# Stationary operands moved to the start address modulo 256 bytes of the moving ones, by sizes of small tiles

## The chip, the cores and the metric

The kernel runs on one core of one Trainium2 chip. The metric is the device time in microseconds (us) of one execution. The engines are TensorE (PE; its weight loads have a row of their own, PEld), VectorE (DVE), ScalarE (ACT), GpSimd (POOL) and SyncE (SP), which issues most of the loads. TensorE has two granted clocks here, 1.2 and 2.4 GHz; a granted clock of 1.00 in the rows is the upper one.

## The reference, cut to what matters

One decoder layer on 256 tokens of width 2048, in float32: a layer norm, one wide projection, three token mixers (a short gated convolution A, a chunked spatial gating B, a conformer convolution C), each projected back and multiplied by a sigmoid gate, an output projection with a residual and a layer norm, and a SwiGLU feed-forward net of inner width 5632 with a residual and a layer norm.

```python
x = layer_norm(x, ln_in_g, ln_in_b)
z = jnp.einsum('bsd,de->bse', x, w_in[l])
a_b, a_c, a_h, b_u, b_v, c_a, c_g, g = jnp.split(z, SPLITS, axis=-1)
gates = jax.nn.sigmoid(g + gate_bias[l]).reshape(bsz, s, N_BRANCH, D_MODEL)
y_a = short_gated_conv(a_b, a_c, a_h, conv_a_w[l])
y_b = chunked_spatial_gating(b_u, b_v, sg_ln_g[l], sg_ln_b[l], sg_w[l], sg_b[l])
y_c = conformer_conv(c_a, c_g, cc_conv_w[l], cc_conv_b[l], cc_ln_g[l], cc_ln_b[l])
proj = jnp.einsum('bsnc,ncd->bsnd', jnp.stack([y_a, y_b, y_c], axis=2), w_branch[l])
mix = jnp.einsum('bsd,de->bse', jnp.sum(gates * proj, axis=2), w_out[l])
x = layer_norm(DEEPNORM_ALPHA * x + mix, ln_mix_g[l], ln_mix_b[l])
h_gate, h_up = jnp.split(jnp.einsum('bsd,df->bsf', x, w_ffn_in[l]), 2, axis=-1)
ffn = jnp.einsum('bsf,fd->bsd', jax.nn.silu(h_gate) * h_up, w_ffn_out[l])
x = layer_norm(DEEPNORM_ALPHA * x + ffn, ln_ffn_g[l], ln_ffn_b[l])
```

## The kernel before

**Products.** Every float32 factor is split into two float32r halves, a high one (ACT casts it, line 127 for weights) and a low one (DVE subtracts, line 129). A product is three matmuls of 128x512 into one PSUM bank: high by high, high by the weights' low, low by the weights' high (lines 197 to 199 in `mm_tile`, 243 to 245 in `product`). The *moving* operand is always a half of a weight tile, `whi` or `wlo`. The *stationary* operand, which a weight load of its own (LDWEIGHTS) brings into the array before each matmul, is a 128x128 block, 512 bytes in each partition, of the transposed activations: `th`/`tl` (halves of the layer's input, of the merged branches, of the normed input of the feed-forward net, of its inner activations), `yh`/`yl` (halves of a mixer's output), and the token sums `sum0`/`sum1` and `xS0`/`xS1`, with which some pairs of blocks are multiplied in seven products in place of eight. Transposes (line 305, `transpose4`) are matmuls of 128x128 by the constant `ident`.

**Stages.** The input projection and the gates read the first `th`/`tl` (to 819 us). Six blocks, one for each half of the output of each branch projection, read `yh`/`yl`. The gate and up projections of the feed-forward net come in three parts, from 819, 1080 and 1336 us, and read the second kind of `th`/`tl`, the list `x2T`, and the sums `xS`. After each part its down projection reads `th`/`tl` and `sum` at the old places. The weights stream through: SP loads them in the order of use, ACT and DVE split them some steps ahead, and PE takes them in program order. Beside that, DVE has a background list (convolution taps, line 558).

**Where tiles lie.** A pool hands out addresses in the order in which its tiles are first asked for, each rounded up to 32 bytes. `brp` (opened in `more_params`) holds what the mixers need: `merged0`, `tok`, `pad`, `cv`, `gate`, the statistics `bst0` and `bst1`, `yh`, `yl`, `merged1`. `ffp` (opened in `open_ffn`, after `brp` and `cwp` are closed) holds `x2T`, the residual `R`, `xS` and the tiles `a`.

Of the kernel before, what the change touches and what calls it, by code (L numbers as in the profile page):

```python
# [8 lines left out]
F32 = mybir.dt.float32  # L9
# [5 lines left out]
P = 128  # L15
D = 2048
S = 256
NT = S // P
DA = D // 2
KC = 31  # L20
# [32 lines left out]
def trunk_kernel(ctx: ExitStack, tc: tile.TileContext, x, ln_in_g, ln_in_b, w_in, gate_bias,  # L53
# [9 lines left out]
    small = ctx.enter_context(tc.tile_pool(name="small", bufs=4))  # L63
# [13 lines left out]
    def cols(j, w=NW):  # L77
        return slice(j * w, (j + 1) * w)

    def new_tmp():  # L80
        return tmp.tile([P, NW], F32, name="tmp")

    def blocks(ap):
        return ap.rearrange("p (b d) -> p b d", d=P)
# [119 lines left out]
    def defer(fn, after=DEFER, banks=True):  # L204


        deferred.append((clock[0] + after, fn, banks))
# [7 lines left out]
    def gemm(key, xs, evac, skew=0):  # L215

        first_tile, nk = chunk[key]
        xh, xl = xs
        ps = [acc_bank() for _ in range(NT)]
        n = nk // KT  # L220
        for i in range(n + skew):
            if i < n:
                pump(first_tile + i)
            for t, ii in ((0, i), (1, i - skew)):
                if not 0 <= ii < n:
                    continue
                hi, lo = split_t[first_tile + ii]
                for kk in range(KT):
                    k = ii * KT + kk
                    mm_tile(ps[t], xh, xl, t, k, hi, lo, kk, k == 0, k == nk - 1)  # L230
                if ii == n - 1:
                    if t == NT - 1:
                        halves.reverse()
                    evac(t, ps[t])
            clock[0] += 1
            run_deferred()
        for i in range(n):
            split_t.pop(first_tile + i)
# [62 lines left out]
    def transpose4(src):  # L301

        tp = tp_bank()
        for b in range(4):
            nc.tensor.transpose(out=tp[:, b, :], in_=src[:, b, :], identity=ident)  # L305
        return tp
# [16 lines left out]
        nc.gpsimd.tensor_tensor(out=rs, in0=r, in1=mhalf, op=ALU.pow)  # L323
        return mv[:, 0:1], rs

    def stats_tile(name, n, pool=None):
        return [(pool or small).tile([P, n, 6], F32, name=f"{name}{t}", bufs=1) for t in range(NT)]


    wi = w_in[0]  # L330
# [79 lines left out]
    def pcol(base, b):  # L410
        return prm[:, base + b:base + b + 1]
# [28 lines left out]
    def new_xt(pool):  # L440
        return (pool.tile([P, 16, S], F32R, name="th"), pool.tile([P, 16, S], F32R, name="tl"))
# [51 lines left out]
    br = ExitStack()  # L493
    brp = None
    cc_tok, cc_stats = [], stats_tile("cst", 2)
    b_ln, wT = [], []

# [28 lines left out]
    def branch_c_chunk(j):  # L526
        sig, st = {}, {}

        def evac_cg(t, ps):
            sig[t] = new_tmp()  # L530
            nc.scalar.activation(out=sig[t], in_=ps, func=AF.Sigmoid)

        gemm(("cg", j), xT, evac_cg, skew=SKEW_IN if j == 0 else 0)

        def evac_ca(t, ps):
            y = new_tmp()
            nc.vector.tensor_tensor(out=y, in0=ps, in1=sig[t], op=ALU.mult)

            def later():
                if t == 0:  # L540
                    st["pad"] = brp.tile([P, 4, KC - 1 + S], F32, name="pad", bufs=2)
                    nc.vector.memset(st["pad"][:, :, 0:KC - 1], 0.0)
                tp = transpose4(blocks(y))
                nc.scalar.copy(out=st["pad"][:, :, KC - 1 + t * P:KC - 1 + (t + 1) * P], in_=tp)
                if t == NT - 1:
                    queue_conv(st["pad"])
            defer(later)

        def queue_conv(pad):
            def tap(q, b):  # L550
                if q == 0 and b == 0:
                    st["cv"] = brp.tile([P, 4, S], F32, name="cv", bufs=2)
                cv, w_ = st["cv"], cw[:, 4 * j + b, q:q + 1]
                if q == 0:
                    nc.vector.tensor_scalar(out=cv[:, b, :], in0=pad[:, b, 0:S], scalar1=w_,
                                            scalar2=pcol(PR_CB, 4 * j + b), op0=ALU.mult, op1=ALU.add)
                else:
                    nc.vector.scalar_tensor_tensor(out=cv[:, b, :], in0=pad[:, b, q:q + S], scalar=w_,  # L558
                                                   in1=cv[:, b, :], op0=ALU.mult, op1=ALU.add)

            def back():
                if not cc_tok:
                    cc_tok.extend(brp.tile([P, DA], F32, name="tok", bufs=2) for _ in range(NT))
                for t in range(NT):
                    tp = transpose4(st["cv"][:, :, cols(t, P)])
                    dst = cc_tok[t][:, cols(j)]
                    nc.scalar.copy(out=blocks(dst), in_=tp)
                    nc.vector.bn_stats(out=cc_stats[t][:, j, :], in_=dst)

            for q in range(KC):  # L570
                for b in range(4):
                    background.append(lambda q=q, b=b: tap(q, b))
            background.append(lambda: defer(back))

        gemm(("ca", j), xT, evac_ca)
# [27 lines left out]


    vt = {(t, j): brp.tile([P, NW], F32, name="gate", bufs=4) for t in range(NT) for j in range(2)}
    bst = stats_tile("bst", 2, brp)
    for j in range(2):
        def evac_bv(t, ps, j=j):
            nc.scalar.copy(out=vt[t, j], in_=ps)
# [36 lines left out]
    def total(ps, add):  # L646

        if add is None:
            return ps
        c = new_tmp()  # L650
        nc.vector.tensor_tensor(out=c, in0=ps, in1=add, op=ALU.add)  # L651
        return c
# [67 lines left out]
    ac, pads, cvs = {}, {}, {}  # L720
# [10 lines left out]
    def evac_ah(i, t, h, ps, add):  # L731
        u = ac[t, h]
        nc.vector.tensor_tensor(out=u, in0=total(ps, add), in1=u, op=ALU.mult)

        def later():
            if h not in pads:
                pads[h] = brp.tile([P, 4, KC - 1 + S], F32, name="pad", bufs=2)
                nc.vector.memset(pads[h][:, :, 0:KA - 1], 0.0)
            pad = pads[h]
            tp = transpose4(blocks(u))  # L740
            nc.scalar.copy(out=pad[:, :, KA - 1 + t * P:KA - 1 + (t + 1) * P], in_=tp)
            if t < NT - 1:
                return
            cv = cvs[h] = brp.tile([P, 4, S], F32, name="cv", bufs=2)
            for q in range(KA):
                for b in range(4):
                    w_ = cw[:, 4 * h + b, KC + q:KC + q + 1]
                    if q == 0:
                        nc.vector.tensor_scalar(out=cv[:, b, :], in0=pad[:, b, 0:S], scalar1=w_,
                                                scalar2=None, op0=ALU.mult)  # L750
                    else:
                        nc.vector.scalar_tensor_tensor(out=cv[:, b, :], in0=pad[:, b, q:q + S], scalar=w_,
                                                       in1=cv[:, b, :], op0=ALU.mult, op1=ALU.add)
        defer(later, DEFER + i)
# [30 lines left out]
    ffp = None  # L785
    R, x2T, xS = [], [], []

    def open_ffn():
        nonlocal ffp
        br.close()  # L790
        cwx.close()
        ffp = ctx.enter_context(tc.tile_pool(name="ffp", bufs=1))
        x2T.extend(new_xt(ffp))
        R.extend(ffp.tile([P, D], F32, name=f"R{t}") for t in range(NT))
        xS.extend(ffp.tile([P, 4, S_PAIRS, P], F32R, name=f"xS{i}") for i in range(2))

    defer(open_ffn, 1)

    def bcast(src, j):
        t_ = new_tmp()  # L800
        nc.gpsimd.dma_start(out=t_, in_=src[0:1, cols(j)].broadcast_to([P, NW]))
        return t_

    stm = stats_tile("stm", 4)
    lg2, lb2 = (a.rearrange("(o d) -> o d", o=1) for a in (ln_in_g, ln_in_b))
    def residual_rows(j):
# [152 lines left out]
```

## Time and profile before

| | before |
|---|---|
| time, median of 3 runs | 1544.6 us (1544.12 to 1544.81) |
| the profiled execution: its time | 1543.98 us |
| its span, first to last instruction | 1541.9 us |
| PE busy | 1522.0 us of the span, 6799 matmuls |
| DVE busy | 1343.1 us |
| ACT busy | 771.6 us |
| mean DMA rate | 200 GB/s |

A matmul's duration in the rows is from its start until its result is complete, and matmuls overlap: one of 389 ns is followed after some 227 ns by the next. So a busy PE says little; what counts is the distance from start to start, and where one group of matmuls is longer than another of the same shape by some nanoseconds, its distance is longer by about as much.

### The profile page before, as it was taken

What the parts mean: (1) busy time and instruction counts of PE and PEld (TensorE: products, weight loads), DVE (VectorE), ACT (ScalarE), POOL (GpSimd) and SP (SyncE); (2) the same over time, 40 slices, a digit from 0 to 9 for tenths busy, and PEclk for the clock granted to TensorE, in tenths of its full rate; (3) what the DMA queues carried; (4) which work ended last, traced back from release to release, by engine and by line L of the source; (5) the groups of instructions that cost most, each with busy time, mean ns of one, the idle gap of its engine ahead of it and who ended that gap; (6) DMA issues with size and microseconds to landing.
All of it is one profiled execution on the core that took longest, in us unless ns stands there. A gap on an engine that the chain in (4) does not pass through costs nothing.

```text
span 1541.9 us, 18855 instructions
## 1 busy us (share of the span) xinstructions
PE 1522.0 (99%) x6799; PEld 1247.5 (81%) x6799; DVE 1343.1 (87%) x1792; ACT 771.6 (50%) x885; POOL 40.6 (3%) x72
## 2 busy tenths in 40 slices
PE   8999999999999999999999999999999999999997
PEld 5888888888888888888887888888888888888885
DVE  7699999978789878778979799998899998889677
ACT  6544445444455454545536455554555554455451
POOL 1000000000000000000101000000000000000001
PEclk9999999999999999999999999999999999999999
DMA  7766657566665655756766666676665656666663
GB/s 240 256 193 190 182 169 231 170 204 198 198 194 177 229 191 166 262 172 219 255 196 181 203 191 219 190 233 198 186 197 172 213 196 204 202 193 197 213 190 124
DMA packets 102549, 308.14 MB, mean 200 GB/s; under 512 B 9909, under 2 KB 11029, under 8 KB 102455
## 3 DMA queue, kind: packets, MB, share of 16 engines
q1 hardware_dynamic: 98006, 293.29, 60.0%
q0 software_dynamic: 3520, 11.54, 2.7%
q10 hardware_dynamic: 928, 2.11, 0.4%
q8 instruction: 53, 0.87, 0.2%
q14 instruction: 42, 0.34, 0.1%
HBM read 304.80 MB, written 2.10 MB: 199 GB/s over the span
## 4 chain that ended last, share of the span: by engine, by line
PE 86%; DVE 9%; issue 2%; DMA 1%; ACT 1%; POOL 0%; POOLq 0%; DVEq 0%; ACTq 0%
PE acc L243 24%; PE acc L245 24%; PE acc L244 24%; DVE cv L558 4%; PE acc L198 4%; PE acc L199 4%; PE acc L197 4%; DVE wlo L129 2%; PE acc L305 2%; DMA wraw<-in_w_in_dram 0%; DMA x<-in_x_dram 0%; POOL ve L320 0%; DVE st L468 0%; DVE tmp L635 0%; ACT whi L127 0%
## 5 line engine op out<-in xcount | busy, mean ns | idle before, releaser
L127 ACT CAST whi<-wraw 128x1024 fp32r<-128x1024 f32 x551 | 575.8, 1052 | 519.8 <-PE acc L245 274.0
L129 DVE TENSOR_TENSOR wlo<-wraw,whi 128x1024 fp32r<-128x1024 f32 x551 | 666.6, 1220 | 125.7 <-ACT whi L127 119.3
L243 PE MATMUL acc<-whi,th 128*128 128x512 f32 x1235 | 485.7, 393 | 0.0
L244 PE MATMUL acc<-wlo,th 128*128 128x512 f32 x1235 | 481.7, 390 | 0.0
L245 PE MATMUL acc<-whi,tl 128*128 128x512 f32 x1235 | 481.1, 390 | 0.0
L245 PEld LDWEIGHTS acc<-whi,tl 128*128 128x128 f32 x1235 | 231.8, 188 | 50.3
L243 PEld LDWEIGHTS acc<-whi,th 128*128 128x128 f32 x1235 | 231.9, 188 | 48.3 <-ACT th L311 0.5
L244 PEld LDWEIGHTS acc<-wlo,th 128*128 128x128 f32 x1235 | 232.1, 188 | 47.8
L197 PE MATMUL acc<-whi,th 128*128 128x512 f32 x496 | 195.1, 394 | 0.1
L199 PE MATMUL acc<-whi,tl 128*128 128x512 f32 x496 | 194.1, 392 | 0.0
L198 PE MATMUL acc<-wlo,th 128*128 128x512 f32 x496 | 193.8, 392 | 0.0
L127 ACT CAST whi<-tsum 128x1024 fp32r<-128x1024 f32 x114 | 95.2, 835 | 153.2 <-DVE tsum L139 98.8
L129 DVE TENSOR_TENSOR wlo<-tsum,whi 128x1024 fp32r<-128x1024 f32 x114 | 108.7, 953 | 20.2 <-ACT whi L127 19.7
L199 PEld LDWEIGHTS acc<-whi,tl 128*128 128x128 f32 x496 | 93.4, 188 | 20.4 <-DVE tl L312 0.8
L197 PEld LDWEIGHTS acc<-whi,th 128*128 128x128 f32 x496 | 93.5, 189 | 19.9 <-ACT th L311 0.6
L198 PEld LDWEIGHTS acc<-wlo,th 128*128 128x128 f32 x496 | 93.4, 188 | 19.4 <-DVE wlo L129 0.2
L558 DVE SCALAR_TENSOR_TENSOR cv<-pad,cw,cv 128x256 f32<-128x256 f32 x240 | 102.0, 486 | 0.0
L139 DVE TENSOR_TENSOR tsum<-tsum,wraw 128x512 f32<-128x512 f32 x114 | 78.1, 685 | 0.7
L243 PE MATMUL acc<-whi,yh 128*128 128x512 f32 x192 | 76.3, 398 | 0.0
L245 PE MATMUL acc<-whi,yl 128*128 128x512 f32 x192 | 75.9, 395 | 0.0
L244 PE MATMUL acc<-wlo,yh 128*128 128x512 f32 x192 | 75.9, 395 | 0.0
L651 DVE TENSOR_TENSOR tmp<-acc,tmp 128x512 f32<-128x512 f32 x92 | 59.9, 683 | 0.6
(164 smaller groups left out, 1178.1 us busy)
## 6 DMA issues: line engine op xcount, KB each, us to landing
wraw<-in_w_in_dram SPq DMA_DIRECT2D x208, 512.0 KB, 4.3
wraw<-in_w_ffn_in_dram SPq DMA_DIRECT2D x176, 512.0 KB, 4.5
wraw<-in_w_ffn_out_dram SPq DMA_DIRECT2D x88, 512.0 KB, 4.7
wraw<-in_w_branch_dram SPq DMA_DIRECT2D x48, 512.0 KB, 5.1
wraw<-in_w_out_dram SPq DMA_DIRECT2D x32, 512.0 KB, 5.8
tmp<-in_gate_bias_dram POOLq DMA_DIRECT2D x12, 256.0 KB, 4.4
R<-in_x_dram POOLq DMA_DIRECT2D x8, 256.0 KB, 8.6
x<-in_x_dram SPq DMA_DIRECT2D x2, 512.0 KB
```

Of the source, the lines that this page charges most:

```text
L127: nc.scalar.copy(out=hi, in_=t)
L129: nc.vector.tensor_tensor(out=lo, in0=t, in1=hi.bitcast(F32), op=ALU.subtract)
L139: nc.vector.tensor_tensor(out=out, in0=a, in1=b, op=ALU.add)
L197: nc.tensor.matmul(ps, lhsT=xh[:, k, ts], rhs=hi[:, kk, :], start=first, stop=False)
L198: nc.tensor.matmul(ps, lhsT=xh[:, k, ts], rhs=lo[:, kk, :], start=False, stop=False)
L199: nc.tensor.matmul(ps, lhsT=xl[:, k, ts], rhs=hi[:, kk, :], start=False, stop=last)
L243: nc.tensor.matmul(ps, lhsT=ah, rhs=bh, start=first, stop=False)
L244: nc.tensor.matmul(ps, lhsT=ah, rhs=bl, start=False, stop=False)
L245: nc.tensor.matmul(ps, lhsT=al, rhs=bh, start=False, stop=last)
L305: nc.tensor.transpose(out=tp[:, b, :], in_=src[:, b, :], identity=ident)
L558: nc.vector.scalar_tensor_tensor(out=cv[:, b, :], in0=pad[:, b, q:q + S], scalar=w_, in1=cv[:, b, :], op0=ALU.mult, op1=ALU.add)
L651: nc.vector.tensor_tensor(out=c, in0=ps, in1=add, op=ALU.add)
```

## The change

Four sizes in the two pools change, so that tiles that come later start elsewhere. No instruction is added or taken out, and the order of the instructions on each engine, the semaphores that they wait for and the shapes that they compute on are those of before. The tiles `pad` have rows of 288 in place of 286 elements, of which the last two aren't used; the two statistics tiles `bst0` and `bst1` (each 48 bytes, rounded up to 64) become slices of one of 256 bytes; `ffp` begins with an unused tile of 64 bytes.

```diff
-    def stats_tile(name, n, pool=None):
-        return [(pool or small).tile([P, n, 6], F32, name=f"{name}{t}", bufs=1) for t in range(NT)]
+    def stats_tile(name, n):
+        return [small.tile([P, n, 6], F32, name=f"{name}{t}", bufs=1) for t in range(NT)]
...
-                    st["pad"] = brp.tile([P, 4, KC - 1 + S], F32, name="pad", bufs=2)
+                    st["pad"] = brp.tile([P, 4, KC + 1 + S], F32, name="pad", bufs=2)
...
-    bst = stats_tile("bst", 2, brp)
+    bst_ = brp.tile([P, 64], F32, name="bst")
+    bst = [bst_[:, 12 * t:12 * t + 12].rearrange("p (j s) -> p j s", s=6) for t in range(NT)]
...
-                pads[h] = brp.tile([P, 4, KC - 1 + S], F32, name="pad", bufs=2)
+                pads[h] = brp.tile([P, 4, KC + 1 + S], F32, name="pad", bufs=2)
...
         ffp = ctx.enter_context(tc.tile_pool(name="ffp", bufs=1))
+        ffp.tile([P, 16], F32, name="align")
         x2T.extend(new_xt(ffp))
```

What that does to the start addresses in a partition, read from the two built programs (in bytes; in brackets modulo 256):

| tile | read by matmuls as | before | after |
|---|---|---|---|
| `whi`, `wlo` | moving | 38080 and on, 66752 and on (192) | same |
| `th`, `tl` outside `x2T` | stationary | 101568, 117952 (192) | same |
| `sum0`, `sum1` | stationary | 134336, 138432 (192) | same |
| `th`, `tl` of `x2T` | stationary | 159616, 176000 (128) | 159680, 176064 (192) |
| `xS0`, `xS1` | stationary | 208768, 214912 (128) | 208832, 214976 (192) |
| `yh`, `yl` | stationary | 202752, 210944 (0) | 202944, 211136 (192) |
| `a` (four buffers) | stationary of transposes | 221056 and on (128) | 221120 and on (192) |
| `merged0` | the same | 160704 (192) | same |
| `merged1` | the same | 219136 (0) | 219328 (192) |
| `gate`, `cv`, `R` | the same | (128) | (192) |
| `ident` | moving of transposes | 16512 (128) | same |

Within a tile the blocks start at multiples of 512 bytes (stationary) and 2048 bytes (moving), so that a tile's place modulo 256 is that of all its blocks.

## Rows read from the trace of the kernel before

**Rows 1.** The page, part 1, and the span with the granted clock.
```profile
PE 1522.0 (99%) x6799; PEld 1247.5 (81%) x6799; DVE 1343.1 (87%) x1792; ACT 771.6 (50%) x885; POOL 40.6 (3%) x72
...
core 0: 1541.9 us, clock 0.996
```
**Rows 2.** Waits of PE, longest first: engine, line, releaser, us, times, longest.
```profile
PE acc L305 <- DVE tmp L427: 5.9, 6, 2.0
```
**Rows 3.** Groups of PE by shape, 270.7 to 312.6 us (gate projection, first th/tl).
```profile
L244 PE MATMUL acc<-wlo,th 128*128 128x512 f32 x54 | 21.0, 389 | 0.0
L243 PE MATMUL acc<-whi,th 128*128 128x512 f32 x54 | 21.0, 389 | 0.0
L245 PE MATMUL acc<-whi,tl 128*128 128x512 f32 x53 | 20.6, 389 | 0.0
```
**Rows 4.** The same, 313 to 335 us (a branch projection, yh/yl).
```profile
L243 PE MATMUL acc<-whi,yh 128*128 128x512 f32 x32 | 12.7, 396 | 0.0
L244 PE MATMUL acc<-wlo,yh 128*128 128x512 f32 x32 | 12.7, 396 | 0.0
L245 PE MATMUL acc<-whi,yl 128*128 128x512 f32 x31 | 12.3, 396 | 0.0
```
**Rows 5.** The same, 1091 to 1166 us (gate and up projections, th/tl of x2T, xS).
```profile
L243 PE MATMUL acc<-whi,th 128*128 128x512 f32 x86 | 33.7, 392 | 0.0
L244 PE MATMUL acc<-wlo,th 128*128 128x512 f32 x85 | 33.5, 394 | 0.0
L245 PE MATMUL acc<-whi,tl 128*128 128x512 f32 x86 | 33.4, 388 | 0.0
L244 PE MATMUL acc<-wlo,xS 128*128 128x512 f32 x24 | 9.5, 394 | 0.0
```
**Rows 6.** Timeline of PE: first matmuls of three blocks (start us, duration us).
```profile
270.72 0.39 PE L243 MATMUL acc<-whi,th 128*128 128x512 f32 x1
...
312.89 0.40 PE L243 MATMUL acc<-whi,yh 128*128 128x512 f32 x1
...
335.29 0.39 PE L243 MATMUL acc<-whi,th 128*128 128x512 f32 x1
```
**Rows 7.** Busy time of PE (count) in the three gate and up stages.
```profile
818.90:993.60 174.70, 174.16 (x775) 1.00 0.64 198
1079.90:1249.30 169.40, 169.40 (x750) 1.00 0.63 197
1335.80:1465.30 129.50, 129.50 (x576) 1.00 0.62 196
```
**Rows 8.** Groups beside transposes: 996.1 to 1009 us, then 1166.2 to 1179 us.
```profile
L243 PE MATMUL acc<-whi,th 128*128 128x512 f32 x17 | 7.0, 414 | 0.0
L244 PE MATMUL acc<-wlo,th 128*128 128x512 f32 x17 | 6.6, 390 | 0.0
...
L243 PE MATMUL acc<-whi,th 128*128 128x512 f32 x17 | 7.0, 415 | 0.0
```
**Rows 9.** Line 702 on DVE (merged0 and merged1): duration ns min/median/max.
```profile
L702 DVE TENSOR_TENSOR merged<-merged,gate x16: 679/682/685, 531.0 to 732.3; 128x512 f32<-128x512 f32 x16
```
**Rows 10.** Busy time: PE, PEld, DVE, ACT, POOL (counts), clock, DMA; late first part.
```profile
885.00:927.00 42.00, 42.00 (x193) 34.55 (x192) 39.33 (x52) 24.28 (x30) 0.00 (x0) 1.00 0.59 182
927.00:970.00 43.00, 43.00 (x189) 35.27 (x189) 41.97 (x52) 23.62 (x27) 2.12 (x4) 1.00 0.71 223
970.00:994.00 24.00, 24.00 (x107) 19.68 (x106) 23.50 (x30) 13.33 (x15) 0.00 (x0) 1.00 0.61 188
```
**Rows 11.** Line 245: the last matmul before transposes of merged0, tmp, a.
```profile
L245 PE MATMUL acc<-whi,tl x1: 393/393/393, 731.0 to 731.0; 128*128 128x512 f32 x1
...
L245 PE MATMUL acc<-whi,tl x1: 393/393/393, 467.2 to 467.2; 128*128 128x512 f32 x1
...
L245 PE MATMUL acc<-whi,tl x1: 400/400/400, 996.2 to 996.2; 128*128 128x512 f32 x1
```
**Rows 12.** Line 244 on the sums at 192, whole span: duration ns min/median/max, first, last.
```profile
L244 PE MATMUL acc<-wlo,sum x120: 389/389/393, 222.1 to 1493.9; 128*128 128x512 f32 x120
```

## The prediction

> **What bounds the kernel now.** I read the page's busy times first, then the waits, then groups of matmuls stage by stage. PE is busy for 1522.0 of 1541.9 us at a granted clock of 0.996 [rows 1], and its longest wait in total is 5.9 us, for the first layer norm [rows 2]; the other engines have idle time. So PE's stream of matmuls sets the time, and the clock is at its upper level in every stage that matters [rows 7, 10]. Within that stream the reader is to see one thing: matmuls of the same shape, on the same moving tiles, without a wait, don't all take the same time. With the first `th`/`tl` as the stationary operand all three forms last 389 ns [rows 3]. With `yh`/`yl` they last 396 ns [rows 4]. With the `th`/`tl` of `x2T` they last 392, 394 and 388 ns, 391.3 on average, and `xS` goes with them (394 for the middle form) [rows 5]. The starts say the same without the modelled end: the 96 matmuls with `yh`/`yl` take from 312.89 to 335.29 us, 233.3 ns from start to start, and the 186 before them from 270.72 to 312.89 us, 226.7 ns [rows 6]. The difference, 6.6 ns, is the 7 ns of the durations.
>
> These three speeds go with the table of addresses: 192 modulo 256 (as the moving tiles) is the fast one, 128 is 2.3 ns slower, 0 is 7 ns slower. That it is the offset and not the region of the memory follows from `xS`: it lies at 208768 to 221055, beside `yh`/`yl` (202752 to 219135), in the same bytes for a good part, and yet it has the speed of `x2T`'s `th` at 159616, with which it shares only the offset. What the trace shows is that the distance goes with the relation of the two addresses; that the load of the next stationary block, which runs beside the current matmul, and that matmul's reads get in each other's way is my reading of it.
>
> **The change part by part.** Nothing is removed or added on any engine; what changes is the distance of two kinds of matmuls.
>
> *The 2031 matmuls on `x2T` and `xS`* (741, 732 and 558 by the program; the three stages hold 775, 750 and 576 matmuls with their transposes and the edges of the windows [rows 7]). Each goes from 391.3 to 389 ns: 2031 x 2.33 = 4.7 us.
>
> *The 576 matmuls on `yh`/`yl`* (six blocks of 96). Each goes from 396 to 389 ns: 576 x 7 = 4.0 us.
>
> *What doesn't gain.* After a group of transposes the matmuls run out of step for some twelve, whatever the alignment. In 996.1 to 1009 us the stationary operand is at 192, in 1166.2 to 1179 us at 128, both with four groups of transposes: the first of the three forms has 414 and 415 ns, and the second, at 192, 390 [rows 8]. So about 50 matmuls for each such place gain nothing: three places in the gate and up stages, some 50 more at their beginning (819 to 834 us, where PE waits for the second layer norm), and about 61 of those on `yh`/`yl` (five groups). The sum is (2031 - 200) x 2.33 = 4.3 us and (576 - 61) x 7 = 3.6 us, together 7.9 us.
>
> *Transposes and the other engines.* `a`, `gate`, `cv` and `R` go from the offset of `ident` to 64 bytes beside it, where `tmp` and `merged0` are already. The matmul that runs while the first block of `merged0` or `tmp` is loaded lasts 393 ns, the one before `a` 400 ns [rows 11]: with about twenty such groups that is 0.1 us of gain at most, and I take nothing. DVE and ACT read the moved tiles too. Line 702 takes 679 to 685 ns over sixteen, of which eight are on `merged0` (192) and eight on `merged1` (0) [rows 9], so I take nothing there either; the ends are the 3 ns to each side of its median times some 300 moved DVE instructions, under 1 us of an engine that isn't on the path. The loads keep size and order.
>
> *What hides it.* No wait stands between PE's stream and the end: all of the 7.9 us come off if the weight halves are ready. Where DVE is busiest, 885 to 994 us, it works 104.8 of 109 us [rows 10], so 4.2 us are idle, and PE will want these halves about 1 us earlier (109 us x 2.33/229). That fits, with little to spare in the last 24 us (23.5 busy).
>
> The sum against the profiled execution: 1543.98 - 7.9 = 1536.1 us, with a span of 1534.0. That execution is 0.6 us under the median of the runs, so against the median 1544.6 - 7.9 = **1536.7 us**.
>
> **The rivals.**
>
> *Nothing moves.* The three speeds would come from the stages and not from the offset, by something that changes with the stage (what DVE, ACT and the loads do there). For it: each offset occurs only in its own stages. Against it: the sums at 192 have 389 ns as their median from 222.1 to 1493.9 us, with 393 as the longest, before, between and after the gate and up stages [rows 12]. It would give 1544.6 us. The Trainium skill speaks for this rival: "TensorE: Matmul & The Clock Gate", section "Step-by-step: what each phase is for", says that the moving operand and the weight load have independent read ports of SBUF, so that loading the next block takes nothing from the running matmul, and "SBUF — State Buffer", section "Who interferes with whom", that PE never waits on anyone. By these pages the addresses would change nothing and the sum would be zero. The 396 against 389 ns [rows 3, 4] don't agree with it, so I give it little.
>
> *The period is 512, not 256 (slower than before).* `x2T` and `xS` at their new places are 256 bytes off the moving tiles modulo 512, a relation that no 128x512 matmul with them has had; `yh`/`yl` land at the same place modulo 512 as the first `th` and are safe. If the relation were bad, up to the worst seen, 7 ns in place of 2.33, it would cost 1831 x 4.67 = 8.5 us against the gain of 3.6: 1544.6 + 4.9 = 1549.5 us. It decides the sign from a price of 2.33 + 3.6/1.831 = 4.3 ns. Against it stands `merged0`, which lies at 448 modulo 512, 256 off the moving tiles: the matmul under its first load takes 393 ns, exactly as the one under `tmp`, at 192 modulo 512, and not 400 as under `a` [rows 11].
>
> *Only the branch projections gain.* A milder form of it: the new relation is as good as the old one, `x2T` keeps its 391.3 ns: 1544.6 - 3.6 = 1541.0 us.
>
> *DVE takes over.* If the splits came late between 885 and 994 us, the about 1.1 us that PE gains there would turn into waits: 1537.8 us.
>
> **How the numbers follow.** A change of 0.2% is 3.1 us, about what a measurement of this kernel can tell from none. The forecast, with sums from 7.0 (the means of 1831 matmuls are rounded by up to 0.5 ns, 0.9 us) to 8.7 us (those beside transposes gain too), has 0.78; DVE takes over 0.08; only the branch projections 0.05; nothing moves 0.05; the period of 512 0.04. Faster: 0.78 + 0.08 + 0.05 = 0.91; same 0.05; slower 0.04. The forecast alone spans 1535.9 to 1537.6, DVE's case adds 1537.8, and the runs of before differ by 0.7 us among themselves, with the profiled one 0.8 us apart; with 1 us to both sides for that the range is 1534.9 to 1538.8, which leaves out the other three, 0.14.
>
> **What would show it.** Right: 389 ns for the `yh`, `xS` and `x2T` groups in stretches without transposes, the blocks on `yh` 21.8 in place of 22.4 us long, the three gate and up stages about 1.4 us shorter each, no new wait in PE's list, and DVE's durations as before. Wrong in the rule: 391 or more in the gate and up stages with `yh` at 389 (the period), or nothing at 389 (another cause). Wrong in the cover: 389 everywhere, but a new wait of PE for `wlo` from 885 to 994 us.

## The result and the profile after

The changed kernel takes 1537.35 us (median of 5 runs, 1536.00 to 1538.31), against 1544.81 us before (median of 5, 1544.12 to 1546.23, the three of the table before among them). The medians are 7.5 us apart. The ratio is 0.9949, with a 95% interval of 0.9937 to 0.9961, so the gain lies between 6.0 and 9.7 us. The prediction was 1536.7 us.

The page after, part 1, and the span with the granted clock:

```profile
PE 1512.8 (98%) x6799; PEld 1247.0 (81%) x6799; DVE 1343.1 (87%) x1792; ACT 770.6 (50%) x885; POOL 40.7 (3%) x72
...
core 0: 1536.0 us, clock 0.995
```

The number of instructions and the busy time of DVE are those of [rows 1]; PE's busy time falls from 1522.0 to 1512.8 us, and no other moves by more than 1.0. Next, the groups of PE by shape in a stretch of a branch projection (316 to 335 us) and in one of the gate and up projections (1091 to 1160 us), which answer to [rows 4] and [rows 5]:

```profile
L243 PE MATMUL acc<-whi,yh 128*128 128x512 f32 x29 | 11.3, 389 | 0.0
L244 PE MATMUL acc<-wlo,yh 128*128 128x512 f32 x29 | 11.3, 389 | 0.0
L245 PE MATMUL acc<-whi,yl 128*128 128x512 f32 x28 | 10.9, 389 | 0.0
...
L244 PE MATMUL acc<-wlo,th 128*128 128x512 f32 x78 | 30.4, 389 | 0.0
L243 PE MATMUL acc<-whi,th 128*128 128x512 f32 x78 | 30.3, 389 | 0.0
L245 PE MATMUL acc<-whi,tl 128*128 128x512 f32 x78 | 30.3, 389 | 0.0
L244 PE MATMUL acc<-wlo,xS 128*128 128x512 f32 x24 | 9.3, 389 | 0.0
```

All that were 396, 392, 394 or 388 are 389 now, the value of [rows 3]. The first matmul of a branch projection and that of the block behind it, on the timeline of PE (start us, duration us):

```profile
314.36 0.39 PE L243 MATMUL acc<-whi,yh 128*128 128x512 f32 x1
...
336.12 0.39 PE L243 MATMUL acc<-whi,th 128*128 128x512 f32 x1
```

The block lasts 21.76 us where [rows 6] have 22.40. Done for each stage, from the start of its first matmul to that of the next stage, this gives:

| stretch, us from start to start | before | after |
|---|---|---|
| six blocks on `yh`/`yl` | 137.03 | 133.36 |
| three gate and up stages | 473.61 | 469.40 |
| the other blocks from the first branch projection on | 672.07 | 671.93 |
| from the span's start to the first branch projection | 247.43 | 249.55 |

The first two lines give 3.67 and 4.21 us, 7.88 together. (PE's busy time fell by 9.2 us: these 7.88, 0.14 in the other blocks and 1.1 before the first branch projection.) The profiled execution's span fell by only 5.9 us, from 1541.9 to 1536.0, because this one execution came to its first branch projection 2.1 us later. PE's waits, longest first, say where:

```profile
PE acc L305 <- DVE tmp L427: 9.0, 5, 5.3
PE acc L418 <- DVE zero L415: 1.3, 1, 1.3
PE acc L305 <- DVE R L427: 1.2, 2, 0.8
PE acc L243 <- DVE yl L312: 0.2, 1, 0.2
PE acc L197 <- ACT th L311: 0.2, 1, 0.2
```

The wait for the first layer norm (line 427) is 9.0 us in place of the 5.9 of [rows 2]. The last two are new, 0.2 us each, and for halves of activations; there is no wait for `wlo`. The order and the work are the same up to there; that stretch differs between executions of all kernels here, as the end of this document shows.

### The profile page after: what moved, and what is told of

It reads as the page before. It is cut to its first block, busy times and chain, and to the rows that moved or that the text cites. A ratio compares the mean times of both kernels' runs of the same rounds, so it can differ in the third digit from the quotient of the medians.

```text
span 1536.0 us, 18855 instructions
## 1 busy us (share of the span) xinstructions
PE 1512.8 (98%) x6799; PEld 1247.0 (81%) x6799; DVE 1343.1 (87%) x1792; ACT 770.6 (50%) x885; POOL 40.7 (3%) x72
## 4 chain that ended last, share of the span: by engine, by line
PE 86%; DVE 9%; issue 3%; DMA 1%; ACT 1%; POOL 0%; SPq 0%; POOLq 0%; DVEq 0%; ACTq 0%
PE acc L243 24%; PE acc L245 24%; PE acc L244 24%; DVE cv L558 4%; PE acc L198 4%; PE acc L199 4%; PE acc L197 4%; DVE wlo L129 2%; PE acc L305 2%; DMA wraw<-in_w_in_dram 1%; DVE tmp L427 0%; POOL ve L320 0%; DVE tmp L636 0%; ACT whi L127 0%; DVE cv L555 0%
```

## The experiments

Each kernel was run beside the kernel before on the same chip. "Offset" is the start of a stationary block less that of the moving tile, modulo 256 bytes. Of the groups of a stretch, some are shown.

**One half alone: `x2T` and `xS`.** The kernel before with the unused tile in `ffp` only.

```diff
         ffp = ctx.enter_context(tc.tile_pool(name="ffp", bufs=1))
+        ffp.tile([P, 16], F32, name="align")
```

> Only the unused tile of 64 bytes at the head of ffp is added: x2T and xS go to 192 modulo 256, yh and yl stay at 0. Theory (the distance between matmuls is set by the start of the stationary block against that of the moving tile, modulo 256): the groups on x2T and xS at 389 ns, those on yh and yl still at 396, the three gate and up stages shorter by 1.3 to 1.5 us each, the time lower by 4.3 us than before. Rival (the speeds belong to the stages or to the region of the memory): 391 to 392 ns on x2T as before, time unchanged. Rival (period of 512): 391 ns or more on x2T, time unchanged or longer.

Measured: 1541.69 us against 1545.29 (18 runs), ratio 0.9977, interval 0.9967 to 0.9987. Groups of PE from 1091 to 1160 us, then from 316 to 335 us:

```profile
L244 PE MATMUL acc<-wlo,th 128*128 128x512 f32 x78 | 30.3, 389 | 0.0
L244 PE MATMUL acc<-wlo,xS 128*128 128x512 f32 x24 | 9.3, 389 | 0.0
...
L243 PE MATMUL acc<-whi,yh 128*128 128x512 f32 x28 | 11.1, 396 | 0.0
```

What was moved is at 389 ns, what was not stays at 396. From start to start the gate and up stages take 469.39 us, 4.22 less than before, and the blocks on `yh`/`yl` the 137.03 of before. `x2T` is 256 off the moving tiles modulo 512 here, and has the full gain: a period of 512 is ruled out.

**The other half: `yh` and `yl`.** The changed kernel without the tile in `ffp`.

```diff
-        ffp.tile([P, 16], F32, name="align")
```

> Only the sizes in brp are changed: yh and yl go to 192 modulo 256, x2T and xS stay at 128. Theory: 389 ns on yh and yl, a block of 96 matmuls 21.8 us long in place of 22.4, 391.3 ns on x2T as before, the time lower by 3.6 us; with the 4.3 us of the other half this adds up to the 7.9 us forecast. Rival (one shared cause, such as DVE or the loads, that caps the gain): the two halves add up to more than the whole change gives, that is over 8.5 us.

Measured: 1541.17 us, ratio 0.9974, interval 0.9966 to 0.9983. The same two stretches:

```profile
L244 PE MATMUL acc<-wlo,th 128*128 128x512 f32 x77 | 30.3, 394 | 0.0
L244 PE MATMUL acc<-wlo,xS 128*128 128x512 f32 x24 | 9.5, 394 | 0.0
...
L243 PE MATMUL acc<-whi,yh 128*128 128x512 f32 x29 | 11.3, 389 | 0.0
```

The mirror image: the blocks take 133.36 us (3.67 less), the gate and up stages 473.54. The medians of the two halves are 3.6 and 4.1 us under before, 7.7 together, where the whole change gives 7.5; from start to start they are 4.22 and 3.67 us against 7.88. They add up, and no shared cause caps them.

**The relation or the place.** The changed kernel with everything 32 bytes further.

```diff
     const = ctx.enter_context(tc.tile_pool(name="const", bufs=1))
+    const.tile([P, 8], F32, name="shift")
```

> The changed kernel with an unused tile of 32 bytes at the very beginning, so that every tile lies 32 bytes further: moving and stationary at 224 modulo 256, still equal. Theory (only the relation counts): 389 ns everywhere, time as the changed kernel, 7.5 us under before. Rival (192 is a good place in itself): the stationary operands leave it, and all matmuls take 391 ns or more, 2.3 ns times 6336 matmuls or 14.6 us over the changed kernel.

Measured: 1536.52 us, ratio 0.9946, interval 0.9933 to 0.9960, as the changed kernel. Groups of PE from 1091 to 1160 us (lines one further down):

```profile
L245 PE MATMUL acc<-wlo,th 128*128 128x512 f32 x79 | 30.7, 389 | 0.0
L246 PE MATMUL acc<-whi,tl 128*128 128x512 f32 x78 | 30.3, 389 | 0.0
```

So 192 has no merit of its own: equal operands at 224 are as good.

**How the price goes with the offset.** Four kernels, in which the sizes of `bst` and of the tile in `ffp` are varied. Shown is the first:

```diff
-    bst_ = brp.tile([P, 64], F32, name="bst")
+    bst_ = brp.tile([P, 72], F32, name="bst")
...
-        ffp.tile([P, 16], F32, name="align")
+        ffp.tile([P, 8], F32, name="align")
```

The others have 88 and 24, 96 and 16, 104 and 16 in these places.

> The changed kernel with yh and yl 32 bytes past the moving tiles (224 modulo 256) and x2T and xS 32 bytes short of them (160). Theory (a graded price: the further off, modulo 256, the dearer, forwards more than backwards): yh and yl between 389 and 396, about 392 ns; x2T between 389 and 391.3, about 390 ns. Rival (any offset but equality costs the same in its direction): 396 on yh and yl, 391.3 on x2T.

> The changed kernel with yh and yl 96 bytes past the moving tiles (32 modulo 256) and x2T and xS 32 bytes past them (224). Theory (graded price): yh and yl at 396 or more, up to 399 ns; x2T about 392 ns, as yh and yl with the same 32 bytes, since the tile and the stage don't count. Rival (same price in one direction): 396 on both. Rival (the stage sets the price): x2T at another value than yh and yl at 32 bytes.

> The changed kernel with yh and yl 128 bytes past the moving tiles, the furthest modulo 256; x2T and xS stay equal. Theory (graded price): the dearest of all, 396 to 403 ns on yh and yl. Rival (a period of 128): 389 ns, as equal. Rival (a place half a period off is the best, since the two streams of reads miss each other): under 389.

> The changed kernel with yh and yl 160 bytes past, or 96 short of, the moving tiles. Theory (graded price): between the price of 128 and the 391.3 ns of 64 short, about 393 ns. Rival (same price in one direction): 391.3.

Measured: 1553.24, 1553.39, 1540.71 and 1542.05 us, one run each beside 1544.63 of before. Groups of PE of the first kernel (offsets 32 and, for `x2T`, 224), 317 to 335 and 1095 to 1160 us:

```profile
L243 PE MATMUL acc<-whi,yh 128*128 128x512 f32 x26 | 10.3, 396 | 0.0
...
L245 PE MATMUL acc<-whi,tl 128*128 128x512 f32 x73 | 28.8, 395 | 0.0
```

The second (96 and 32):

```profile
L245 PE MATMUL acc<-whi,yl 128*128 128x512 f32 x26 | 10.3, 397 | 0.0
...
L245 PE MATMUL acc<-whi,tl 128*128 128x512 f32 x73 | 28.9, 396 | 0.0
```

The third (128), `yh` only:

```profile
L243 PE MATMUL acc<-whi,yh 128*128 128x512 f32 x27 | 10.7, 395 | 0.0
L244 PE MATMUL acc<-wlo,yh 128*128 128x512 f32 x27 | 10.6, 394 | 0.0
```

The fourth (160):

```profile
L244 PE MATMUL acc<-wlo,yh 128*128 128x512 f32 x26 | 10.4, 399 | 0.0
L243 PE MATMUL acc<-whi,yh 128*128 128x512 f32 x26 | 10.2, 394 | 0.0
L245 PE MATMUL acc<-whi,yl 128*128 128x512 f32 x26 | 10.2, 392 | 0.0
```

| offset | 0 | 32 | 64 | 96 | 128 | 160 | 192 | 224 |
|---|---|---|---|---|---|---|---|---|
| duration by form, ns | 389 | 396 | 396 | 396 to 397 | 394 to 395 | 392 to 399 | 388 to 394 | 395 |
| from start to start, mean, ns | 226.7 | 233.3 | 233.3 | 234.3 | 232.4 | 233.3 | 228.9 | 233.3 |

(64 and 192 are those of the kernel before [rows 4, 5]; the second line is from the starts of matmuls in stretches without transposes.) The graded price falls: 32 bytes to either side cost as much as 64 forwards, and of the unequal multiples of 32 that were tried only 192, where `x2T` was, is clearly cheaper. The rest are within 2 ns of each other, so the rivals with one price for each direction fall as well, by 224 and 160. A period of 128, and a best place half a period off, fall too. `x2T` and `yh` at the same offset of 32 have the same price, 233.3 ns from start to start, so tile, stage and region of the memory play no visible part in it. The kernels with `x2T` at 32 and 224 are 9 us slower than before: what was an accident of sizes could have fallen worse.

**Sixteen bytes, and four.** `yh` and `yl` get longer tiles, of which a later part is used; 4 elements in the first kernel, 1 in the second.

```diff
-        return (brp.tile([P, 8, S], F32R, name="yh"), brp.tile([P, 8, S], F32R, name="yl"))
+        y_ = [brp.tile([P, 64 + 8 * S], F32R, name=n) for n in ("yh", "yl")]
+        return tuple(y[:, 4:4 + 8 * S].rearrange("p (k s) -> p k s", s=S) for y in y_)
```

> yh and yl 16 bytes past the moving tiles modulo 256, all else as in the changed kernel. Theory (any inequality costs, as 32 bytes cost 6.6 ns with either tile): 393 to 396 ns on yh and yl, 2.5 to 4 us over the changed kernel. Rival (a line of 32 bytes is the grain, so that 16 bytes are still equal): 389 ns.

> yh and yl one element, 4 bytes, past the moving tiles modulo 256, all else as in the changed kernel. Theory (the streams only have to stay within one line of 16 or 32 bytes): between 389 and 392 ns on yh and yl. Rival (equality to the byte): 393 to 396 ns.

Measured: 1537.12 us with 16 bytes, 1540.65 with 4 (before: 1544.28), one run each. Groups of PE from 315 to 335 us, first with 16 bytes:

```profile
L243 PE MATMUL acc<-whi,yh 128*128 128x512 f32 x29 | 11.3, 389 | 0.0
L244 PE MATMUL acc<-wlo,yh 128*128 128x512 f32 x29 | 11.3, 389 | 0.0
```

The same with 4 bytes:

```profile
L243 PE MATMUL acc<-whi,yh 128*128 128x512 f32 x29 | 11.4, 394 | 0.0
L244 PE MATMUL acc<-wlo,yh 128*128 128x512 f32 x29 | 11.4, 394 | 0.0
```

Both theories fall, each to its rival. In this stretch sixteen bytes off is as good as equal (389), and four bytes off costs 5 ns, so the price doesn't grow with the distance. Whether 4 bytes cost by the same mechanism as 32, or by one of their own, these runs don't say.

But sixteen bytes are not equality. In the sixth block, which has four groups of transposes, the matmuls with 16 bytes don't come back into step after the last of them (720 to 724.8 us):

```profile
L245 PE MATMUL acc<-whi,yl 128*128 128x512 f32 x8 | 3.2, 394 | 0.0
L243 PE MATMUL acc<-whi,yh 128*128 128x512 f32 x7 | 2.8, 397 | 0.0
L244 PE MATMUL acc<-wlo,yh 128*128 128x512 f32 x7 | 2.8, 395 | 0.0
```

The same place of the changed kernel (721 to 725.8 us):

```profile
L243 PE MATMUL acc<-whi,yh 128*128 128x512 f32 x7 | 2.7, 389 | 0.0
L244 PE MATMUL acc<-wlo,yh 128*128 128x512 f32 x8 | 3.1, 389 | 0.0
```

With 16 bytes they go on at 233.3 ns from start to start up to the end of the block, where equal operands are back at 226.7 after some twelve. So one offset has both speeds in one kernel, by what went before: the offset alone doesn't set the price, the state of the stream does too.

**Which of the two loads is in the way.** Only `yl` off by 64 bytes, then only `yh`.

```diff
-        return (brp.tile([P, 8, S], F32R, name="yh"), brp.tile([P, 8, S], F32R, name="yl"))
+        yh = brp.tile([P, 8, S], F32R, name="yh")
+        yl = brp.tile([P, 16 + 8 * S], F32R, name="yl")
+        return (yh, yl[:, 16:].rearrange("p (k s) -> p k s", s=S))
...
+        yh = brp.tile([P, 64 + 8 * S], F32R, name="yh")
+        yl = brp.tile([P, 8, S], F32R, name="yl")
+        return (yh[:, 16:16 + 8 * S].rearrange("p (k s) -> p k s", s=S), yl)
```

> The changed kernel with yl alone moved by 64 bytes against the moving tiles (0 modulo 256), yh at 192. Matmuls come as whi by yh (line 243), wlo by yh (244), whi by yl (245). Theory (the load of the next stationary block gets in the way of the running matmul): line 244, beside which yl is loaded, is the long one, at 396 ns or more, and lines 243 and 245, beside which yh is loaded, stay near 389 to 392. Rival (a matmul is slow by its own stationary block): line 245 is the long one, 396, and 243 and 244 have 389.

> The counterpart of the kernel in which yl alone was moved (389.0, 391.9 and 397.3 ns on lines 243, 244 and 245): here yh is 64 bytes past the moving tiles and yl equal. If a matmul is slow by its own stationary block: lines 243 and 244 long, at 394 to 398 ns, line 245 at 389 to 391. If it is slow by the load of the next block, which stands beside it in the trace: lines 243 and 245 long, line 244 short.

Measured: 1538.46 us with `yl` off, 1541.24 with `yh` off (one run each; the kernel before took 1545.29, the median of 18 runs, beside the first, and 1544.28, one run, beside the second). Groups of PE from 315 to 335 us with `yl` off:

```profile
L245 PE MATMUL acc<-whi,yl 128*128 128x512 f32 x30 | 11.9, 397 | 0.0
L244 PE MATMUL acc<-wlo,yh 128*128 128x512 f32 x29 | 11.4, 392 | 0.0
L243 PE MATMUL acc<-whi,yh 128*128 128x512 f32 x29 | 11.3, 389 | 0.0
```

The same with `yh` off:

```profile
L243 PE MATMUL acc<-whi,yh 128*128 128x512 f32 x30 | 11.9, 398 | 0.0
L245 PE MATMUL acc<-whi,yl 128*128 128x512 f32 x29 | 11.5, 397 | 0.0
L244 PE MATMUL acc<-wlo,yh 128*128 128x512 f32 x29 | 11.4, 392 | 0.0
```

The first kernel goes more with "by its own stationary block" (line 245 is the long one, though 244 has 392 and not 389), the second with "by the load of the next" (243 and 245 long, 244 short). Neither reading explains both. A matmul on line 244 with its own block equal and the next off has 392 in the first kernel, one on line 245 in the same position has 397 in the second: so the price of one matmul isn't a function of its own block and the next alone, and something is carried along the stream. The blocks' totals are simpler: from the starts, a block of 96 matmuls takes 21.76 us with all equal, 22.18 with one stationary operand in three off, 22.40 with two in three off and 22.40 with all off [rows 6]. The third costs nothing more. One count gives all four: 6.7 ns for each matmul whose own block or the next one is off, which are none, two in three, all and all. (The own block or the one before gives the same.) It is fitted to these totals and says nothing of how the price is spread over the lines, so it isn't shown as the mechanism.

That the address of the next block alone can lengthen a running matmul is shown at another place. The matmul before a group of transposes of `a`, at 996.2 us, its own block at 192, took 400 ns while `a` lay at 128 [rows 11]. With `a` at 192 it takes 393, in the changed kernel:

```profile
L245 PE MATMUL acc<-whi,tl x1: 393/393/393, 993.0 to 993.0; 128*128 128x512 f32 x1
```

It has 393 in the kernel with `ffp` alone moved, too, and 400 in the one with `brp` alone, in which `a` stays at 128. So a matmul isn't slow by its own block only. Which reads collide, and what is carried along, stays open.

**All operands off.** The changed kernel with 32 bytes at the head of the pool from which the first `th`/`tl`, the sums and all later pools follow, but not the weights.

```diff
+    act.tile([P, 8], F32, name="shift")
     xT = new_xt(act)
```

> The changed kernel with an unused tile of 32 bytes at the head of the pool act, so that every stationary operand of a 128x512 product, the first th and tl and the sums too, lies 32 bytes past the moving tiles. Theory (the price per matmul adds up over the whole stream and nothing hides it): 395.5 ns everywhere, 6.6 ns times 6336 matmuls less the some 500 beside transposes, 38 to 42 us over the changed kernel, 1575 to 1579 us. Rival (part of the price is hidden where PE runs close to DVE): under 30 us over it.

Measured: 1576.47 us, 39.1 over the changed kernel's median, as the theory had it. The page's part 1:

```profile
PE 1552.0 (99%) x6799; PEld 1247.9 (79%) x6799; DVE 1349.9 (86%) x1792; ACT 771.3 (49%) x885; POOL 40.9 (3%) x72
```

Groups of PE from 275 to 312 us, which are 389 in [rows 3]:

```profile
L243 PE MATMUL acc<-whi,th 128*128 128x512 f32 x42 | 16.6, 396 | 0.0
L244 PE MATMUL acc<-wlo,th 128*128 128x512 f32 x41 | 16.2, 396 | 0.0
L243 PE MATMUL acc<-whi,sum 128*128 128x512 f32 x8 | 3.2, 396 | 0.0
```

PE's busy time rises by 39.2 us, from 1512.8 to 1552.0, and the time with it. The whole price is on the path; the kernel before paid 7.9 us of such a price, since most of its operands were equal.

## Why the prediction was right

*What bounds the kernel.* Right: PE's busy time and the time moved together in every kernel, to some 3 us, and no wait of PE for a weight half appeared in any.

*`x2T` and `xS`.* Forecast 4.3 us after taking off what stands beside transposes, measured 4.21 from start to start. "About 1.4 us" for each stage was 1.46, 1.56 and 1.18.

*`yh` and `yl`.* Forecast 3.6, measured 3.67; a block 21.8 and 21.76.

*How near the sums came is partly luck.* They go by durations, 2.33 and 7 ns a matmul (the 396 of the rows is 395.5, rounded); from start to start it is 2.2 (228.9 to 226.7) and 6.7 (233.3 to 226.7). The prediction had read 6.6 itself, and its sum took the 7. The other way, it took off too many matmuls: the measured gains are those of some 1900 and 550 matmuls at the full gain, where the sums have 1831 and 515. The two errors, of some 5% each, nearly cancel.

*Beside transposes.* Held by the durations: 1162.5 to 1175.3 us, the place of [rows 8] with its operand now equal, has 414, 389 and 393 ns in the three forms; [rows 8] have 415 for the first of them there, and 414 and 390 for the first two where the operand was equal before. "Gain nothing" was too strong: from start to start each of the three places of the gate and up stages became 0.03 to 0.05 us shorter, where 51 matmuls with the full gain would give 0.11, and the sixth block gained half of it beside its transposes.

*The other engines and the cover.* DVE's busy time is the same to the tenth. In 885 to 994 us DVE has 105.0 of 109 us busy and PE waits for nothing there:

```profile
927.00:970.00 43.00, 43.00 (x191) 35.62 (x190) 41.80 (x53) 23.49 (x29) 2.12 (x4) 1.00 0.72 220
970.00:994.00 24.00, 24.00 (x110) 19.89 (x109) 23.49 (x30) 14.63 (x18) 0.00 (x0) 1.00 0.67 216
```

PE passes 191 and 110 matmuls where [rows 10] have 189 and 107, with DVE as busy as before; a part of that is that the same window holds work some 2.5 us further on.

*The rivals.* "Nothing moves" fell by the two halves, each of which moved its own stages alone. Of the two pages of the Trainium skill that spoke for it, "TensorE: Matmul & The Clock Gate", section "Step-by-step: what each phase is for", says that loading the next block takes nothing from the running matmul; these runs don't agree, with 389 against 396 ns for one shape on one tile by its start address alone, and 393 against 400 by that of the next block. "SBUF — State Buffer", section "Who interferes with whom", says that PE waits on nobody; that is on one engine and another, and these runs, which change PE's own two operands, don't test it. The period of 512, and with it a gain of the branch projections only, fell by `x2T`, whose place is 256 off modulo 512. DVE didn't take over. The forecast's size, 7.9 us, is the 7.88 of the stages; the median's 7.5 us differs from it by less than the runs of either kernel differ among themselves.

*What was only my reading.* The prediction offered the load of the next block as what gets in the way, and marked it as a reading. The matmul before the transposes of `a` bears it out (400 to 393 ns); the two kernels with one operand off don't in that simple form. The sum didn't rest on it. Nor would a gradual price between the known offsets, which I expected later, have been right.

## What to carry to other kernels

Where PE's stream sets the time, compare the mean durations of matmuls of one shape on different stationary tiles: a few nanoseconds between groups, without a wait, times thousands is a term worth a look at the addresses. Let stationary and moving operands of float32r products start at the same address modulo 256 bytes; in this kernel any other multiple of 32 cost 2 to 8 ns of some 227 for each matmul, and 16 bytes off cost 6.7 ns once transposes had put the stream out of step. And since small tiles decide where later ones start, a change that is meant for something else can move the time this way, here by 39 us, 2.5%, from the best to the worst that was tried; look at start addresses before explaining such a difference by the change itself.

## What the runs showed that was not expected

An offset of 16 bytes was as good as none (389 ns) until transposes broke the stream, and had the full price from there to the end of the block (394 to 397); one of 4 bytes cost 5 ns (394), and one of 32 had the full price (396).

With equal operands it is 226.7 ns from start to start, which are 544 cycles of the upper clock of 2.4 GHz for 512 columns. What the 32 beyond one for each column are was not tried.

The beginning varies by itself. On the timeline of DVE the first two instructions that write normed input take 1.00 us in the profiled execution before:

```profile
8.90 1.00 DVE L427 TENSOR_SCALAR tmp<-x,mvin,rsin 128x512 f32<-128x512 f32 x2 [1.01 <-POOL rsin L323]
```

The same two after, 3.15 us:

```profile
9.38 3.15 DVE L427 TENSOR_SCALAR tmp<-x,mvin,rsin 128x512 f32<-128x512 f32 x2 [1.00 <-POOL rsin L323]
```

Up to the first branch projection the profiled executions took between 247.4 and 249.8 us with the same work (the kernel with all operands off left aside), the one in which everything is 32 bytes further 247.8. That is of the size by which the runs of one kernel differ, 3.5 us between the 18 of before. Its cause was not looked for.
